# Two matmuls with a gelu between them: contraction rows dealt to partitions in fours, and later transposes

## The chip, the cores and the metric

The kernel runs on one core of one Trainium2 chip. The core has a matrix engine (TensorE, PE in the profile, with its weight loads shown apart as PEld), a vector engine (VectorE, DVE), a scalar engine (ScalarE, ACT), GpSimd (POOL) and SyncE (SP). Data move between the device's memory and the core's on-chip memory by DMA. Two queues issue these DMAs here: SP's, for copies without a change of type, and POOL's, for copies that turn fp32 into bf16 (or to the type fp32r) on the way. The metric is the device time of one execution in microseconds.

## The reference

```python
m, k, n, p = 1024, 1024, 2048, 1024      # a: m x k, b: k x n, c: n x p, all fp32
h = np.matmul(a, b)
h = 0.5 * h * (1 + np.tanh(np.sqrt(2 / np.pi) * (h + 0.044715 * h ** 3)))
return np.matmul(h, c).astype(np.float32)
```

## The kernel before, in words

TensorE multiplies a stationary tile of 128 x 128 (the weights) with a moving tile of 128 x 512; both have the contraction in their 128 partitions. So `h` transposed is computed with tiles of `b` as weights and the transpose of `a` as the moving side: 8 slices of the contraction (`KT`), 16 tiles of columns of `b` (`NT`), and two halves of 512 rows of `a`. Each tile of `h` is the sum of 8 matmuls in one bank of PSUM (the matmul's output memory), and ScalarE takes it through the gelu to on-chip memory. The order of instructions on every engine is the order in which the code writes them.

**First half of the rows.** It has three blocks of columns. *Block 0* is tiles 0 to 5. SP loads `a` by slice (`load_a0`, L74 to L78: 128 or 256 columns of the four row tiles) and `b` by slice (`load_b0`, L80 to L83: 128 rows, 768 columns), in the order of L86 to L89. Per slice, VectorE casts the four 128 x 128 pieces of `a` to bf16 (L107), TensorE transposes them (L110), VectorE copies the result into `aT` (L111), and ScalarE casts the slice of `b` in two halves (L113). The six matmuls of the slice before (`mm0`, L100) stand behind the transposes in TensorE's order. Ten matmuls on zeros (L96) come first of all. *Block 1* is tiles 6 to 9: POOL loads `b` in four DMAs of two slices each (`load_b`, L125 and L130), after a small copy, `gate` (L91), has waited for slice 5 of block 0. *Block 2* is tiles 10 to 15: POOL loads it in four DMAs of four slices and 384 columns, and then the four row tiles of the second half of `a` (L155). `mm1` (L139) computes one tile. After each of the tiles 11 to 14, `turn` (L158) transposes one of the four row tiles, in eight transposes into one PSUM tile and one copy by VectorE (L163). The PSUM tiles of all transposes come from a pool with two buffers (`tpool`).

**Second half of the rows.** The same 16 tiles with `aT[1]`, all data being on chip. POOL loads `c` meanwhile, as four quarters in two DMAs each (L184); `c12` takes the place of `aT[0]`, and so can't be loaded before the first half ends.

**Second product.** It is computed by a scheme of seven block products in place of eight, with sums and differences of blocks of `c` and of `h` that VectorE makes during the second half (`sum_t1`, `sum_t2`, `sum_s1` and others). `t1` uses the buffers of the loaded `a`, `t2` those of the loaded `b`. `prod` (L240) issues eight matmuls per output tile; VectorE combines the results, and SP stores them. The very last output tile is computed in two pieces of 256 columns (L307 to L313).

Where the code names slice `k`, its 128 contraction rows are `k * 128` to `k * 128 + 127`, one in each partition. `b` is addressed through `bv` (L35), and `a` through `av` (L34).

Of the kernel before, what the change touches and what calls it, by code (L numbers as in the profile page):

```python
# [9 lines left out]
F32 = mybir.dt.float32  # L10
BF16 = mybir.dt.bfloat16
F32R = mybir.dt.float32r
SUB = mybir.AluOpType.subtract
ADD = mybir.AluOpType.add
AF = mybir.ActivationFunctionType
# [4 lines left out]
def kernel(ctx, tc, a, b, c, out):  # L20
    nc = tc.nc
    M, K = a.shape
    _, N = b.shape
    _, P = c.shape
    KT = K // 128
    NT = N // 128
    MT = M // 128
    H = 512
    N0 = 6
    W0 = N0 * 128  # L30
    N1 = 4
    W1 = N1 * 128

    av = a.rearrange("(mt p) k -> p mt k", p=128)  # L34
    bv = b.rearrange("(kt p) n -> p kt n", p=128)  # L35
    cv = c.rearrange("(nt p) q -> p nt q", p=128)

    ctx.enter_context(tc.manual_schedule())
    consts = ctx.enter_context(tc.tile_pool(name="consts", bufs=1))
    keep = ctx.enter_context(tc.tile_pool(name="keep", bufs=1))  # L40
    astage = ctx.enter_context(tc.tile_pool(name="astage", bufs=4))
    abf = ctx.enter_context(tc.tile_pool(name="abf", bufs=4))
    b0stage = ctx.enter_context(tc.tile_pool(name="b0stage", bufs=8))
    opool = ctx.enter_context(tc.tile_pool(name="opool", bufs=4))
# [1 line left out]
    tpool = ctx.enter_context(tc.tile_pool(name="tpool", bufs=2, space=PSUM))  # L46
# [3 lines left out]
    ident = consts.tile([128, 128], BF16, name="ident")  # L50
# [3 lines left out]
    aT = [keep.tile([128, KT, H], BF16, name=f"aT{h}", tag=f"A{h}") for h in range(2)]  # L54
    WB = W0 + W1
    b_lo = keep.tile([128, KT, WB], BF16, name="b_lo", tag="B0")
    b_hi = keep.tile([128, KT, N - WB], BF16, name="b_hi", tag="B1")

    def bcols(k0, kn, n0, w):
        if n0 < WB:  # L60
            return b_lo[:, k0:k0 + kn, ds(n0, w)]
        return b_hi[:, k0:k0 + kn, ds(n0 - WB, w)]

    def bt(k, t):
        return bcols(k, 1, t * 128, 128)[:, 0, :]
# [5 lines left out]

    a_st, b_st = {}, {}

    def load_a0(k, n):  # L74
        st = astage.tile([128, 4, 256], F32, name="a_st")
        nc.sync.dma_start(out=st[:, :, 0:n * 128], in_=av[:, 0:4, ds(k * 128, n * 128)])  # L76
        for i in range(n):
            a_st[k + i] = st[:, :, ts(i, 128)]  # L78

    def load_b0(k):  # L80
        st = b0stage.tile([128, W0], F32, name="b0_st")
        nc.sync.dma_start(out=st, in_=bv[:, k, 0:W0])  # L82
        b_st[k] = st  # L83

    gate = consts.tile([128, 1], F32, name="gate")
    for k, n in ((0, 1), (1, 1), (2, 2), (4, 2), (6, 2)):  # L86
        load_a0(k, n)
        for i in range(n):
            load_b0(k + i)  # L89

    nc.gpsimd.tensor_copy(gate, b_st[5][:, 0:1])  # L91
    g = consts.tile([128, 1], F32, name="g")
# [4 lines left out]

    ps = [ppool.tile([128, H], F32, name="ps") for _ in range(N0)]

    def mm0(k):  # L100
        for t in range(N0):
            nc.tensor.matmul(ps[t], bt(k, t), aT[0][:, k, :],  # L102
                             start=(k == 0), stop=(k == KT - 1))

    for k in range(KT):
        ab = abf.tile([128, 4, 128], BF16, name="ab")
        nc.vector.tensor_copy(ab, a_st[k])  # L107
        pt = tpool.tile([128, H], BF16, name="pt")
        for j in range(4):
            nc.tensor.transpose(pt[:, ts(j, 128)], ab[:, j, :], ident)  # L110
        nc.vector.tensor_copy(aT[0][:, k, :], pt)  # L111
        for i in range(2):
            nc.scalar.activation(b_lo[:, k, ts(i, W0 // 2)], b_st[k][:, ts(i, W0 // 2)], AF.Copy)  # L113
        if k > 0:
            mm0(k - 1)
    mm0(KT - 1)

    def gelu(t, h, p):
        nc.scalar.activation(hq[h][t // NH][:, t % NH, :], p, AF.Gelu_apprx_tanh)  # L119
# [3 lines left out]


    def load_b(k0, kn, n0, w):  # L125
        nc.gpsimd.dma_start(out=bcols(k0, kn, n0, w), in_=bv[:, k0:k0 + kn, ds(n0, w)])  # L126

    ps = [(tpool if t < 2 else ppool).tile([128, H], F32, name="pt" if t < 2 else "ps")
          for t in range(N1)]
    for k in range(0, KT, 2):  # L130
        load_b(k, 2, W0, W1)
        for i in range(2):
            for t in range(N1):
                nc.tensor.matmul(ps[t], bt(k + i, N0 + t), aT[0][:, k + i, :],
                                 start=(k + i == 0), stop=(k + i == KT - 1))
# [4 lines left out]
    def mm1(t, h):  # L140
        p = ppool.tile([128, H], F32, name="ps")
        for k in range(KT):
            nc.tensor.matmul(p, bt(k, t), aT[h][:, k, :],  # L143
                             start=(k == 0), stop=(k == KT - 1))
        gelu(t, h, p)

    W2 = 384
    for n0 in range(W0 + W1, N, W2):
        for k in range(0, KT, 4):
            load_b(k, 4, n0, W2)  # L150

    a1 = []
    for j in range(4):
        st = abf.tile([128, K], BF16, name="ab1")
# [3 lines left out]
    def turn(j):  # L158
        ab = a1[j]
        pt = tpool.tile([128, KT, 128], BF16, name="pt")  # L160
        for k in range(KT):
            nc.tensor.transpose(pt[:, k, :], ab[:, ts(k, 128)], ident)  # L162
        nc.vector.tensor_copy(aT[1][:, :, ts(j, 128)], pt)  # L163

    for t in range(N0 + N1, NT):
        mm1(t, 0)
        if NT - 5 <= t < NT - 1:
            turn(t - (NT - 5))

# [5 lines left out]
    c11 = keep.tile([128, NH, H], BF16, name="c11")  # L177
    c21 = keep.tile([128, NH, H], BF16, name="c21")
    c22 = keep.tile([128, NH, H], F32R, name="c22")
    c12 = keep.tile([128, NH, H], BF16, name="c12", tag="A0")  # L180
# [7 lines left out]
    load_c(c21, 1, 0)  # L188
    load_c(c12, 0, 1)

    t1 = [astage.tile([128, 2, H], F32R, name="t1", tag="a_st") for _ in range(4)]
    t2 = [b0stage.tile([128, 1, H], F32R, name="t2", tag="b0_st") for _ in range(8)]
    s1 = keep.tile([128, NH, H], F32R, name="s1")

    def sum_t1(i):
        nc.vector.tensor_tensor(t1[i], c12[:, ts(i, 2), :], c11[:, ts(i, 2), :], op=SUB)  # L196

    def sum_t2(t):
        nc.vector.tensor_tensor(t2[t], c22[:, t:t + 1, :], t1[t // 2][:, t % 2:t % 2 + 1, :], op=SUB)

    def sum_s1(t):
        nc.vector.tensor_tensor(s1[:, t, :], h21[:, t, :], h22[:, t, :], op=ADD)
# [1 line left out]
    for t in range(NT):  # L204
        mm1(t, 1)
        if 3 <= t < 7:
            sum_t1(t - 3)
        if 6 <= t < 10:
            sum_t2(2 * (t - 6))
            sum_t2(2 * (t - 6) + 1)  # L210
        if t == WB // 128:
            t3 = keep.tile([128, NH, H], F32R, name="t3", tag="B0")
        if t >= NH + 1:
            sum_s1(t - NH - 1)
        if WB // 128 <= t < WB // 128 + 4:
            i = t - WB // 128
            nc.vector.tensor_tensor(t3[:, ts(i, 2), :], c22[:, ts(i, 2), :], c12[:, ts(i, 2), :], op=SUB)
# [16 lines left out]
    def sum_t4(t):  # L234
        nc.vector.tensor_tensor(t2[t], t2[t], c21[:, t:t + 1, :], op=SUB)

    def bank(w=H):
        return ppool.tile([128, w], F32, name="ps", padded_shape=[128, H])

    def prod(p, lhs, rhs, j, q=slice(0, H)):  # L240
        for t in range(NH):
            nc.tensor.matmul(p, lhs(t)[:, ts(j, 128)], rhs(t)[:, q],  # L242
                             start=(t == 0), stop=(t == NH - 1))

    def whole(x):
        return lambda t: x[:, t, :]
# [1 line left out]
    def halves(x):  # L248
        return lambda t: x[t // 4][:, t % 4, :]

    def pairs(x):
        return lambda t: x[t // 2][:, t % 2, :]

    def ones(x):
        return lambda t: x[t][:, 0, :]

    def new_out():
        return opool.tile([128, H], F32, name="ot")

    def store(ot, m, q0, w=H):  # L260
        nc.sync.dma_start(out=out[ts(m, 128), ds(q0, w)], in_=ot[:, 0:w])

    def combine(m, q, p, u, op=ADD, swap=False):
        ot = new_out()
        nc.vector.tensor_tensor(ot, u if swap else p, p if swap else u, op=op)  # L265
        store(ot, m, q * H)
# [5 lines left out]
    for j in R:  # L272
        p = bank()
        prod(p, whole(h11), whole(c11), j)
        nc.scalar.activation(u2[j], p, AF.Copy)  # L275
    for j in range(3):
        p = bank()
# [3 lines left out]
    last_keep = opool.tile([128, H], F32, name="lk", bufs=1)  # L281
    nc.gpsimd.tensor_copy(last_keep, last)  # L282
    for j in R:
        p = bank()
        prod(p, halves(s2), ones(t2), j)
        nc.vector.tensor_tensor(u2[j], p, u2[j], op=ADD)
    for j in R:
        p = bank()
# [2 lines left out]
        sum_s4(j)  # L291
    for j in R:
        p = bank()
        prod(p, whole(s1), pairs(t1), j)
        combine(4 + j, 1, p, u3[:, j, :])
        nc.vector.tensor_tensor(u2[j], p, u2[j], op=ADD)
        sum_t4(2 * j)
        sum_t4(2 * j + 1)
    for j in R:
        p = bank()  # L300
        prod(p, halves(s2), whole(c22), j)
        combine(j, 1, p, u2[j])
    for j in R:
        p = bank()
        prod(p, whole(h22), ones(t2), j)
        combine(4 + j, 0, p, u3[:, j, :], op=SUB, swap=True)
    for q in range(2):  # L307
        w = H // 2
        p = bank(w)
        prod(p, whole(h12), whole(c21), 3, q=ds(q * w, w))  # L310
        ot = new_out()
        nc.vector.tensor_tensor(ot[:, 0:w], p, last_keep[:, ds(q * w, w)], op=ADD)  # L312
        store(ot, 3, q * w, w)  # L313

# [1 line left out]
_INS = ['a', 'b', 'c']  # L316
# [26 lines left out]
```

## Time and profile before

| | |
|---|---|
| median of 13 runs | 126.64 us (125.19 to 128.81) |
| time of the profiled execution | 128.38 us |
| its span, first to last instruction | 126.6 us |
| PE busy | 116.6 us (92%) |
| DVE busy | 65.4 us (52%) |
| ACT busy | 29.6 us (23%) |
| DMA of SP's queue (`q1`) | 9.44 MB |
| DMA of POOL's queue (`q0`) | 8.91 MB |

A line of the timeline gives the start and length in microseconds, the engine, the line of the code, the operation, and output and input with the number of instructions; in brackets stands how long the engine was idle before it and what ended that. The chain of work that ended last is followed back from the last instruction, at each step to what released it. A line of the windows gives the busy time of the engines in a stretch, in the order PE, PEld, DVE, ACT, POOL, each with its number of instructions, and then the clock granted to TensorE as a share of the full one, the busy share of the DMA engines and their GB/s.

### The profile page before, as it was taken

What the parts mean: (1) busy time and instruction counts of PE and PEld (TensorE: products, weight loads), DVE (VectorE), ACT (ScalarE), POOL (GpSimd) and SP (SyncE); (2) the same over time, 40 slices, a digit from 0 to 9 for tenths busy, and PEclk for the clock granted to TensorE, in tenths of its full rate; (3) what the DMA queues carried; (4) which work ended last, traced back from release to release, by engine and by line L of the source; (5) the groups of instructions that cost most, each with busy time, mean ns of one, the idle gap of its engine ahead of it and who ended that gap; (6) DMA issues with size and microseconds to landing.
All of it is one profiled execution on the core that took longest, in us unless ns stands there. A gap on an engine that the chain in (4) does not pass through costs nothing.

```text
span 126.6 us, 1439 instructions
## 1 busy us (share of the span) xinstructions
PE 116.6 (92%) x555; PEld 67.6 (53%) x562; DVE 65.4 (52%) x94; ACT 29.6 (23%) x54; POOL 19.9 (16%) x28
## 2 busy tenths in 40 slices
PE   6759999999299999999999999999999999999990
PEld 2224545444045544444444444458888888888860
DVE  0223551000022300008999999997449999974340
ACT  4144456507101322333322333100000000000000
POOL 2000099333440040000000000590000000000000
PEclk9986999999968999999999999999999999999999
DMA  3799999999999999992000000006000022344433
GB/s 111 201 383 377 376 280 155 177 203 204 211 206 206 349 376 216 206 206 42 0 3 0 0 5 0 0 0 224 25 0 0 5 83 83 137 175 185 166 127 122
DMA packets 14245, 18.43 MB, mean 146 GB/s; under 512 B 800, under 2 KB 9760, under 8 KB 14240
## 3 DMA queue, kind: packets, MB, share of 16 engines
q0 software_dynamic: 8000, 8.91, 38.8%
q1 hardware_dynamic: 6240, 9.44, 21.1%
q8 instruction: 4, 0.07, 0.2%
q14 instruction: 1, 0.01, 0.0%
HBM read 20.97 MB, written 4.19 MB: 199 GB/s over the span
## 4 chain that ended last, share of the span: by engine, by line
PE 69%; DMA 18%; POOL 5%; SPq 4%; issue 1%; DVE 0%
PE ps L242 40%; PE ps L143 28%; DMA ab<-in_a_dram 11%; DMA b_st<-in_b_dram 7%; POOL b_lo L126 2%; POOL b_hi L126 2%; SPq L82 2%; SPq L76 2%; PE pt L162 2%; DVE ot L312 0%; POOL gate L91 0%
## 5 line engine op out<-in xcount | busy, mean ns | idle before, releaser
L119 ACT ACTIVATE h<-ps 128x512 fp32r<-128x512 f32 (+1 forms) x30 | 17.3, 602 | 31.4 <-PE ps L143 29.0
L143 PE MATMUL ps<-aT,b_hi 128*128 128x512 bf16 x93 | 23.1, 396 | 0.3 <-issue 0.2
L143 PE MATMUL ps<-aT,b_lo 128*128 128x512 bf16 x79 | 17.4, 379 | 0.1
L143 PEld LDWEIGHTS <-b_hi 128*128 128x128 bf16 x96 | 9.5, 101 | 11.4 <-issue 1.4
L242 PE MATMUL ps<-t,s 128*128 128x512 f32 x64 | 15.1, 393 | 0.0
L242 PE MATMUL ps<-t,h 128*128 128x512 f32 x64 | 14.8, 389 | 0.0
L242 PE MATMUL ps<-c,h 128*128 128x512 bf16 (+1 forms) x71 | 14.1, 355 | 0.1
L163 DVE COPY aT<-pt 128x1024 bf16<-128x1024 bf16 x4 | 2.8, 691 | 21.8 <-PE pt L162 21.8
L242 PEld LDWEIGHTS ps<-t,s 128*128 128x128 f32 x64 | 12.0, 188 | 2.6
L242 PEld LDWEIGHTS ps<-t,h 128*128 128x128 f32 x64 | 12.0, 188 | 2.5
L102 PE MATMUL ps<-aT,b_lo 128*128 128x512 bf16 x47 | 13.0, 417 | 0.1
L143 PEld LDWEIGHTS <-b_lo 128*128 128x128 bf16 x80 | 7.8, 98 | 9.4
L196 DVE TENSOR_TENSOR t<-c,c 128x1024 fp32r<-128x1024 bf16 x4 | 4.7, 1222 | 12.9 <-DMA c<-in_c_dram 12.7
L242 PEld LDWEIGHTS <-h 128*128 128x128 bf16 x72 | 6.9, 98 | 7.0 <-issue 0.3
L282 POOL COPY lk<-u 128x512 f32<-128x512 f32 x1 | 5.1, 5079 | 33.5 <-ACT u L275 33.5
L113 ACT ACTIVATE b_lo<-b_st 128x384 bf16<-128x384 f32 x16 | 7.5, 514 | 10.1 <-DMA b_st<-in_b_dram 9.9
L184 POOL DMA_DIRECT2D c<-in_c_dram x8 | 5.9, 743 | 14.2 <-PE ps L143 8.5
L265 DVE TENSOR_TENSOR ot<-ps,u 128x512 f32<-128x512 f32 x11 | 7.3, 683 | 1.1 <-PE ps L242 1.1
L242 PE MATMUL ps<-c,s 128*128 128x512 f32 x32 | 7.4, 389 | 0.0
L102 PEld LDWEIGHTS <-b_lo 128*128 128x128 bf16 x48 | 4.8, 106 | 4.8 <-issue 1.3
L242 PEld LDWEIGHTS ps<-c,s 128*128 128x128 f32 x32 | 6.0, 188 | 1.2
L111 DVE COPY aT<-pt 128x512 bf16<-128x512 bf16 x8 | 3.4, 424 | 6.3 <-PE pt L110 6.3
(37 smaller groups left out, 92.6 us busy)
## 6 DMA issues: line engine op xcount, KB each, us to landing
out_dram<-ot SPq DMA_DIRECT2D x15, 256.0 KB, 2.1
b_st<-in_b_dram SPq DMA_DIRECT2D x8, 384.0 KB, 8.5
c<-in_c_dram POOLq DMA_DIRECT2D x6, 512.0 KB, 13.4
c<-in_c_dram POOLq DMA_DIRECT2D x2, 1024.0 KB, 14.8
a_st<-in_a_dram SPq DMA_DIRECT2D x3, 512.0 KB, 9.0
b_hi<-in_b_dram POOLq DMA_DIRECT2D x4, 384.0 KB, 11.0
b_lo<-in_b_dram POOLq DMA_DIRECT2D x4, 256.0 KB, 6.3
ab<-in_a_dram POOLq DMA_DIRECT2D x4, 256.0 KB, 13.2
```

The lines of the kernel that those rows point to most:

```text
L102: nc.tensor.matmul(ps[t], bt(k, t), aT[0][:, k, :], start=(k == 0), stop=(k == KT - 1))
L111: nc.vector.tensor_copy(aT[0][:, k, :], pt)
L113: nc.scalar.activation(b_lo[:, k, ts(i, W0 // 2)], b_st[k][:, ts(i, W0 // 2)], AF.Copy)
L119: nc.scalar.activation(hq[h][t // NH][:, t % NH, :], p, AF.Gelu_apprx_tanh)
L126: nc.gpsimd.dma_start(out=bcols(k0, kn, n0, w), in_=bv[:, k0:k0 + kn, ds(n0, w)])
L143: nc.tensor.matmul(p, bt(k, t), aT[h][:, k, :], start=(k == 0), stop=(k == KT - 1))
L163: nc.vector.tensor_copy(aT[1][:, :, ts(j, 128)], pt)
L184: nc.gpsimd.dma_start(out=dst[:, t:t + 4, :], in_=cv[:, r * NH + t:r * NH + t + 4, ts(q, H)])
L196: nc.vector.tensor_tensor(t1[i], c12[:, ts(i, 2), :], c11[:, ts(i, 2), :], op=SUB)
L242: nc.tensor.matmul(p, lhs(t)[:, ts(j, 128)], rhs(t)[:, q], start=(t == 0), stop=(t == NH - 1))
L265: nc.vector.tensor_tensor(ot, u if swap else p, p if swap else u, op=op)
L282: nc.gpsimd.tensor_copy(last_keep, last)
```

## The change

- **Contraction rows dealt in fours.** Slice `k` = 4`g` + `r` now takes the rows 512`g` + 4`p` + `r` for the partitions `p` = 0 to 127. Any assignment of the rows will do as long as `a` and `b` have the same one. For `b` this changes `bv`. For `a` it means that a transpose takes every fourth column of a half row (`strided`).
- **Loads of block 0.** `a` is loaded by half rows: eight DMAs, one per half `g` and row tile `mt`, 128 x 512 elements, into eight buffers for four. They come in another order: the four of the first half, b0, b1, two of the second half, b2, the other two, b3 to b7.
- **Transposes of block 0.** `turn0(g, mt)` casts one such load, transposes its four slices, and copies them to `aT`. All four of the first half precede the first matmul; the four of the second half stand inside the matmuls of slices 1 and 2, after the third and the sixth matmul.
- **Casts of `b` in block 0.** VectorE casts 384 of the 768 columns and ScalarE the others, where ScalarE did both. The casts for slices 2 and 3 are written behind the matmuls and transposes of slices 1 and 2, the others ahead of the slice before.
- **Block 1.** Two DMAs of four slices for four of two.
- **Second half of `a`.** `turn(0)` comes after tile 13 and the other three after tile 14.
- **`t1`** has eight tiles of 512 columns for four of two times 512, and as many subtractions.
- **The last output tile** is cut into 384 and 128 columns.

```diff
-    bv = b.rearrange("(kt p) n -> p kt n", p=128)
+    bv = b.rearrange("(g p r) n -> p g r n", p=128, r=4)
-    astage = ctx.enter_context(tc.tile_pool(name="astage", bufs=4))
+    astage = ctx.enter_context(tc.tile_pool(name="astage", bufs=8))
...
-    def load_a0(k, n):
-        st = astage.tile([128, 4, 256], F32, name="a_st")
-        nc.sync.dma_start(out=st[:, :, 0:n * 128], in_=av[:, 0:4, ds(k * 128, n * 128)])
-        for i in range(n):
-            a_st[k + i] = st[:, :, ts(i, 128)]
+    def load_a0(g, mt):
+        st = astage.tile([128, 512], F32, name="a_st")
+        nc.sync.dma_start(out=st, in_=av[:, mt, ts(g, 512)])
+        a_st[g, mt] = st
...
-        nc.sync.dma_start(out=st, in_=bv[:, k, 0:W0])
+        nc.sync.dma_start(out=st, in_=bv[:, k // 4, k % 4, 0:W0])
...
-    for k, n in ((0, 1), (1, 1), (2, 2), (4, 2), (6, 2)):
-        load_a0(k, n)
-        for i in range(n):
-            load_b0(k + i)
+    for mt in range(4):
+        load_a0(0, mt)
+    load_b0(0)
+    load_b0(1)
+    load_a0(1, 0)
+    load_a0(1, 1)
+    load_b0(2)
+    load_a0(1, 2)
+    load_a0(1, 3)
+    for k in range(3, KT):
+        load_b0(k)
...
-    def mm0(k):
+    def strided(x, r):
+        return x.rearrange("p (c r) -> p r c", r=4)[:, r, :]
+
+    def turn0(g, mt):
+        ab = abf.tile([128, 512], BF16, name="ab")
+        nc.vector.tensor_copy(ab, a_st[g, mt])
+        pt = tpool.tile([128, 4, 128], BF16, name="pt")
+        for r in range(4):
+            nc.tensor.transpose(pt[:, r, :], strided(ab, r), ident)
+        nc.vector.tensor_copy(aT[0][:, ts(g, 4), ts(mt, 128)], pt)
+
+    HW = W0 // 2
+
+    def cast_b0(k):
+        nc.vector.tensor_copy(b_lo[:, k, 0:HW], b_st[k][:, 0:HW])
+        nc.scalar.activation(b_lo[:, k, HW:W0], b_st[k][:, HW:W0], AF.Copy)
+
+    for mt in range(4):
+        turn0(0, mt)
+    cast_b0(0)
+    for k in range(KT):
+        if k + 1 < KT and k not in (1, 2):
+            cast_b0(k + 1)
         for t in range(N0):
             nc.tensor.matmul(ps[t], bt(k, t), aT[0][:, k, :],
                              start=(k == 0), stop=(k == KT - 1))
-
-    for k in range(KT):
-        ab = abf.tile([128, 4, 128], BF16, name="ab")
-        nc.vector.tensor_copy(ab, a_st[k])
-        pt = tpool.tile([128, H], BF16, name="pt")
-        for j in range(4):
-            nc.tensor.transpose(pt[:, ts(j, 128)], ab[:, j, :], ident)
-        nc.vector.tensor_copy(aT[0][:, k, :], pt)
-        for i in range(2):
-            nc.scalar.activation(b_lo[:, k, ts(i, W0 // 2)], b_st[k][:, ts(i, W0 // 2)], AF.Copy)
-        if k > 0:
-            mm0(k - 1)
-    mm0(KT - 1)
+            if k in (1, 2) and t in (2, 5):
+                turn0(1, 2 * (k - 1) + t // 3)
+        if k in (1, 2):
+            cast_b0(k + 1)
...
-        nc.gpsimd.dma_start(out=bcols(k0, kn, n0, w), in_=bv[:, k0:k0 + kn, ds(n0, w)])
+        nc.gpsimd.dma_start(out=bcols(k0, kn, n0, w), in_=bv[:, k0 // 4, k0 % 4:k0 % 4 + kn, ds(n0, w)])
...
-    for k in range(0, KT, 2):
-        load_b(k, 2, W0, W1)
-        for i in range(2):
+    for k in range(0, KT, 4):
+        load_b(k, 4, W0, W1)
+        for i in range(4):
...
-            nc.tensor.transpose(pt[:, k, :], ab[:, ts(k, 128)], ident)
+            nc.tensor.transpose(pt[:, k, :], strided(ab[:, ts(k // 4, 512)], k % 4), ident)
...
-        if NT - 5 <= t < NT - 1:
-            turn(t - (NT - 5))
+        if t == NT - 3:
+            turn(0)
+        if t == NT - 2:
+            turn(1)
+            turn(2)
+            turn(3)
...
-    t1 = [astage.tile([128, 2, H], F32R, name="t1", tag="a_st") for _ in range(4)]
+    t1 = [astage.tile([128, 1, H], F32R, name="t1", tag="a_st") for _ in range(8)]
...
     def sum_t1(i):
-        nc.vector.tensor_tensor(t1[i], c12[:, ts(i, 2), :], c11[:, ts(i, 2), :], op=SUB)
+        for t in (2 * i, 2 * i + 1):
+            nc.vector.tensor_tensor(t1[t], c12[:, t:t + 1, :], c11[:, t:t + 1, :], op=SUB)
...
-    for q in range(2):
-        w = H // 2
+    for q0, w in ((0, 384), (384, 128)):
         p = bank(w)
-        prod(p, whole(h12), whole(c21), 3, q=ds(q * w, w))
+        prod(p, whole(h12), whole(c21), 3, q=ds(q0, w))
         ot = new_out()
-        nc.vector.tensor_tensor(ot[:, 0:w], p, last_keep[:, ds(q * w, w)], op=ADD)
-        store(ot, 3, q * w, w)
+        nc.vector.tensor_tensor(ot[:, 0:w], p, last_keep[:, ds(q0, w)], op=ADD)
+        store(ot, 3, q0, w)
```

## The prediction

> **What bounds the kernel now.** I first read the chain of work that ended last. From 34.83 us on it is TensorE without a break; before that it is a load of `a`:
>
> ```profile
> 21.54 13.29 DMA ab<-in_a_dram
> 34.83 0.05 issue
> 34.88 0.62 PE pt L162 x8
> 35.50 1.11 PE ps L143 x3
> ```
>
> Columns: start, length, what. The transposes of the second half of `a` (L162) wait for a load issued at 21.54. From there to the last matmul TensorE is full, so a shift of the end of the first half (45.05, first weights of the second half) shifts the end by as much.
>
> Second, TensorE's timeline of the start and of that wait:
>
> ```profile
> 5.13 0.39 PE L110 MATMUL pt<-ident,ab 128*128 128x128 bf16 x4
> 7.83 0.40 PE L110 MATMUL pt<-ident,ab 128*128 128x128 bf16 x4 [2.31 <-DVE ab L107]
> 8.07 2.59 PE L102 MATMUL ps<-aT,b_lo 128*128 128x512 bf16 x6
> ...
> 19.26 2.75 PE L102 MATMUL ps<-aT,b_lo 128*128 128x512 bf16 x12
> 21.85 0.59 PE L134 MATMUL pt<-aT,b_lo 128*128 128x512 bf16 x2
> ...
> 34.88 0.62 PE L162 MATMUL pt<-ident,ab 128*128 128x128 bf16 x8 [2.31 <-DMA ab<-in_a_dram]
> ```
>
> The first block runs from 8.07 to 21.85, the second starts at 21.85, and TensorE is idle 2.31 us before 34.88.
>
> Third, windows of 3.41 us around the clock's changes (busy times, then the granted clock):
>
> ```profile
> 4.82:8.24 3.42, 1.11 (x11) 0.64 (x10) 0.85 (x2) 0.94 (x2) 0.00 (x0) 1.00 0.92 302
> 8.24:11.65 3.41, 3.41 (x12) 1.31 (x11) 1.36 (x4) 1.59 (x4) 0.00 (x0) 0.50 1.06 390
> 32.13:35.54 3.41, 1.10 (x12) 0.56 (x10) 0.00 (x1) 0.60 (x1) 1.74 (x3) 1.00 1.13 209
> 35.54:38.96 3.42, 3.20 (x11) 1.48 (x11) 0.69 (x1) 0.18 (x1) 1.06 (x2) 0.50 1.18 206
> ```
>
> Twice a window with TensorE busy 1.1 of 3.4 us is followed by one at half clock. A matmul of 512 columns is then 0.427 us apart from the next, else 0.216 (8 in 1.73), so such a window costs up to 1.7 us.
>
> Fourth, VectorE's timeline, for the change puts work there:
>
> ```profile
> 13.54 0.43 DVE L107 CAST ab<-a_st 128x512 bf16<-128x512 f32 x1
> 14.51 0.42 DVE L111 COPY aT<-pt 128x512 bf16<-128x512 bf16 x1 [0.55 <-PE pt L110]
> 14.85 0.42 DVE L107 CAST ab<-a_st 128x512 bf16<-128x512 f32 x1
> ```
>
> The casts at 13.54 and 14.85 read one and the same load; the second could have run at 13.97, but stands behind the copy, which waits for TensorE. One round is 0.48 (cast to transposes) + 0.43 (to the copy; 0.65 at half clock) + 0.35 (to the next cast) = 1.26 us.
>
> **What the Trainium skill says.** "TensorE: Matmul & The Clock Gate", Part 1, states a free-running window of 3413 ns whose idleness halves the clock; the windows above agree. The same page, "Architectural detail", has VectorE and ScalarE as strict FIFO; the cast at 14.85 agrees. "SBUF — State Buffer", Door 1, has 16-byte lines, read at full rate with two hits per line: a step of four bf16 just keeps that. The clock page, "Weight-path perf modes", allows the fast weight load with a column step. No strided weight load is in this trace.
>
> **The change, part by part.** The sum is against the profiled execution: span 126.6, its time 128.38, so 1.78 around it. The median is 126.64, 1.74 below, about one half-clock window.
>
> *Loads of `a` and `b`.* Four loads of 256 KB (2 KB rows) precede b0, so the first matmul needs 1.05 + 0.39 = 1.44 MB instead of 0.26 + 0.39. The windows of four us moved 131 and 267 GB/s, 0.52 MB by 4 us and 1.59 MB by 8: the 1.44 MB are in by 7.5, about 7.9 with landing; the four `a` loads by 6.7. Total bytes are unchanged. SP issues 16 loads for 13, at 0.33 to 0.85 each, ahead of the data; with eight stage buffers it no longer waits for a cast. Each is needed later than it lands, as follows.
>
> *The start.* All four transpose rounds now precede the first matmul. The first transposes follow the ten warm-up matmuls, at 5.13 as now; copy at 5.56. Then cast 5.91, transposes 6.39, copy 6.82; cast 7.17, transposes 7.65, copy 8.08; cast 8.43, transposes 8.91, copy (half clock) 9.56. Behind it VectorE casts its half of b0 at 9.91: 384 columns, by the row of 0.43 us for 512 with some 0.15 fixed, 0.36 us (0.3 to 0.43). The first matmul starts at 9.91 + 0.36 + 0.05 = 10.3, not 8.07. Needed loads are 1 us or more early, so the VectorE queue sets this, not the DMA.
>
> *Slices 1 to 3.* Nine matmuls (1.94) lead to the first late transposes. From there everything alternates through VectorE's queue, because the cast of b2 stands behind the copy of the second round and that of b3 behind the fourth: copy 0.43, cast 0.35, transposes 0.48, copy 0.43, b2 cast 0.35, matmul 0.41, three matmuls 0.65, copy 0.43, cast 0.35, transposes 0.48, copy 0.43, b3 cast 0.35, matmul 0.41 = 5.55. Slices 3 to 7 are 30 × 0.216 = 6.48. Sum 13.97, of which 48 × 0.216 + 4 × 0.22 = 11.25 are work and 2.7 are new stalls of TensorE. ScalarE has 8 casts for 16 (0.51 each), no gain on this path.
>
> *Clock.* From 5.5 to 10.3 TensorE has three bursts of 0.4 us, as little as the window that lost the clock. It restarts at half clock for 0.6 to 4.0 us by the phase of the window (if some 40% busy releases it; the trace bounds that only between 33% and full): 0.3 to 2.0 us lost, 1.15 taken. The second block starts at 10.3 + 13.97 + 1.15 = 25.4 instead of 21.85.
>
> *Second block of `b`.* POOL issues two loads for four; by the b_hi row 0.79 each against 4 × 0.76, 1.4 us less ahead of the ten that follow. Its gate, b5, has 0.52 MB more ahead of it, up to 1.4 us later; with b6 and b7 (0.79 MB, 2.1 us) still moving the engines stay fed, so what follows lands 0 to 1.4 us later. The present last b_lo load is issued at 17.89 and takes up to 8.3: 26.2, so 26.2 to 27.6 against a need at 25.4 + 3.46 = 28.9. Priced at nothing, covered by TensorE being late; without that cover up to 1.4 us.
>
> *Late transposes.* `turn(0)` comes at 25.4 + 6.91 + 4 × 1.73 = 39.2. Its load lands at 34.83 (to 36.2): the wait of 2.31 and the half clock after it (some 1.8) go. In its place the third of three adjacent turns needs a transpose bank: transposes to copy 0.66, copy 0.69, 0.05, against 0.90 of transposing: 0.5 us of stall. First half ends at 25.4 + 6.91 (32 × 0.216) + 10.37 (48) + 4 × 0.45 + 0.5 = 45.0, against 45.05: 3.6 us lost at the start, 3.6 won here.
>
> *Rest.* t1 in eight tiles: two subtractions pitch 0.61 each for one of 1.18, +0.2 us of VectorE; its s2 sums end at 80.7, over 4 us before TensorE wants them, so nothing (0.2 without that cover). The last store split 384 and 128: final VectorE work 0.29 instead of 0.42, but the store before it (0.33 of SP) now starts 0.35 us before the final one is ready: −0.1 to +0.1, taken 0.
>
> Sum: 128.38 − 0.05 = 128.3 us.
>
> **The rivals.** *Faster:* VectorE's queue is no bound, because casts run ahead of copies. Then the start is the loads': second block at 22.8 (last b_lo load 26.2 less 3.46), first half over at 42.4, 125.7 us. It decides where the second block starts before 23.1. For it: four `ab` buffers and two banks would allow it. Against: the cast at 14.85 kept its place. *Same:* the clock never falls, since bursts of transposes may count differently at another phase: first matmul 10.1, second block 24.1, end 127.0. Against: the window at 4.82. *Slower still:* strided weights load at half rate, as fp32 ones do (188 ns against 98); a transpose would then be 0.11 apart instead of 0.056, 0.22 per group on eight groups and 0.45 on four turns: +3.6, 131.9 at most. *The loads bind:* `b` rows of neighbouring partitions lie 32 KB apart instead of 8; against the needs above they would have to be 2 us later than now, and then cost 1 us, 129.3.
>
> **How the numbers follow.** Likeliest 66%, 128.3, own range 127.5 to 129.1. Faster 9%, 125.7. Same 13%, 127.0 (126.3 to 127.3). Strided loads 8% and late loads 4%, 129.2 to 131.9. The range 127.0 to 129.9 leaves out the faster case, half of the same case, and most of the strided one. A change under 0.5% (126.0 to 127.3) can hardly be told from none: faster 0.09, same 0.13, slower 0.78.
>
> **What the profile after would show.** Right: first matmul of the first block near 10.3 with VectorE, not a DMA, named ahead of it; rounds 1.26 apart; waits of TensorE on VectorE in slices 1 to 3; second block near 25; no wait on `ab` in L162, but about 0.5 us before the last turn. Wrong: casts back to back, transposes longer than 0.45 for eight, or TensorE waiting for `b_st` or `b_lo`. A median under 127.3 would refute the start's price.

## The result and the profile after

The changed kernel is slower: 129.63 us in the median (129.14 to 130.98, 11 runs) against 126.44 us for the kernel before (48 runs), a ratio of 1.0285 with a 95% interval of 1.0253 to 1.0317. Its profiled execution took 130.12 us, with a span of 128.2 us. The forecast had the direction and the mechanism; its size, 128.3 us, was 1.3 us short of the median. Some executions of the kernel before, its profiled one (128.38 us) among them, take about 2 us longer than the others, and the ratios here leave such long executions out.

The chain of work that ended last, in the kernel after (start, length, what). No load stands in it any more; at the start it alternates between TensorE and VectorE:

```profile
6.01 0.42 DVE aT L116
6.43 0.34 DVE ab L112
6.78 0.05 issue
6.83 0.43 PE pt L115 x4
...
10.36 0.36 DVE b_lo L121
10.72 0.05 issue
10.76 4.02 PE ps L131 x9
```

TensorE's timeline after, for the start and for the late transposes:

```profile
5.43 0.54 PE L115 MATMUL pt<-ident,ab 128*128 128x128 bf16 x4
6.83 0.41 PE L115 MATMUL pt<-ident,ab 128*128 128x128 bf16 x4 [0.85 <-DVE ab L112]
8.09 0.42 PE L115 MATMUL pt<-ident,ab 128*128 128x128 bf16 x4 [0.85 <-DVE ab L112]
9.36 0.62 PE L115 MATMUL pt<-ident,ab 128*128 128x128 bf16 x4 [0.85 <-DVE ab L112]
10.76 4.02 PE L131 MATMUL ps<-aT,b_lo 128*128 128x512 bf16 x9 [0.79 <-DVE b_lo L121]
...
17.43 0.82 PE L131 MATMUL ps<-aT,b_lo 128*128 128x512 bf16 x3 [0.90 <-DVE b_lo L121]
...
20.53 6.65 PE L131 MATMUL ps<-aT,b_lo 128*128 128x512 bf16 x30 [0.79 <-DVE b_lo L121]
27.01 0.59 PE L154 MATMUL pt<-aT,b_lo 128*128 128x512 bf16 x2
...
43.00 1.06 PE L182 MATMUL pt<-ident,ab 128*128 128x128 bf16 x16
44.39 0.61 PE L182 MATMUL pt<-ident,ab 128*128 128x128 bf16 x8 [0.34 <-DVE aT L183]
44.84 1.89 PE L163 MATMUL ps<-aT,b_hi 128*128 128x512 bf16 x8
```

The rounds of transposes are 1.26 us apart, each behind a cast of VectorE. The first matmul of block 0 is at 10.76 (8.07 before), block 1 begins at 27.01 (21.85 before), and the transposes of the second half of `a` wait for no load. So 5.16 us are lost up to block 1. From there to the end of the first half nearly 3.9 are won: the matmuls of its last tile begin at 44.84 here, 1.3 us later than in the kernel before:

```profile
43.54 1.89 PE L143 MATMUL ps<-aT,b_hi 128*128 128x512 bf16 x7
```

The windows of 3.41 us around the clock's changes, after (busy time and number on PE, PEld, DVE, ACT, POOL; then the granted clock):

```profile
5.74:9.16 3.42, 1.06 (x12) 0.57 (x9) 2.13 (x6) 0.52 (x1) 0.00 (x0) 1.00 0.98 341
9.16:12.57 3.41, 2.42 (x9) 1.07 (x10) 1.44 (x5) 1.04 (x2) 0.00 (x0) 0.50 1.04 409
12.57:15.98 3.41, 3.41 (x13) 1.37 (x11) 0.73 (x2) 1.04 (x2) 0.00 (x0) 0.50 1.02 398
15.98:19.40 3.42, 2.26 (x16) 1.13 (x16) 1.92 (x6) 1.57 (x3) 3.19 (x5) 1.00 0.71 148
```

The clock was halved for two windows in a row, so the first nine matmuls took 4.02 us. VectorE's timeline after shows why its work stands where it does:

```profile
15.25 0.43 DVE L116 COPY aT<-pt 128x512 bf16<-128x512 bf16 x1 [3.94 <-PE pt L115]
...
16.56 0.42 DVE L116 COPY aT<-pt 128x512 bf16<-128x512 bf16 x1 [0.55 <-PE pt L115]
16.90 0.47 DVE L121 CAST b_lo<-b_st 128x384 bf16<-128x384 f32 x1
17.29 0.41 DVE L112 CAST ab<-a_st 128x512 bf16<-128x512 f32 x1
```

The cast of b2 runs at 16.90 behind a copy. ScalarE began its half of the same slice at 11.89, as soon as the load was in; VectorE's half could have run then too, for VectorE was idle 3.94 us before its copy at 15.25, behind which the cast was written.

### The profile page after: what moved, and what is told of

Same layout as the page of the kernel before. It is cut to its first block, busy times and chain, and to the rows that moved or that the text cites. A ratio compares the mean times of both kernels' runs of the same rounds, so it can differ in the third digit from the quotient of the medians.

```text
span 128.2 us, 1442 instructions
## 1 busy us (share of the span) xinstructions
PE 117.4 (92%) x555; PEld 68.0 (53%) x562; DVE 67.6 (53%) x106; ACT 26.3 (21%) x46; POOL 16.9 (13%) x26
## 4 chain that ended last, share of the span: by engine, by line
PE 91%; DVE 4%; issue 2%; DVEq 0%
PE ps L267 39%; PE ps L163 29%; PE ps L131 10%; PE pt L103 3%; PE ps L154 3%; PE pt L154 3%; PE pt L115 2%; DVE aT L116 2%; PE pt L182 1%; DVE ab L112 1%; DVE b_lo L121 1%; DVE aT L183 1%; DVEq L359 0%; DVE warm L50 0%; DVE ot L333 0%
## 5 line engine op out<-in xcount | busy, mean ns | idle before, releaser
L139 ACT ACTIVATE h<-ps 128x512 fp32r<-128x512 f32 (+1 forms) x30 | 17.3, 602 | 33.8 <-PE ps L163 25.2
L163 PE MATMUL ps<-aT,b_hi 128*128 128x512 bf16 x94 | 21.1, 379 | 0.1
L163 PE MATMUL ps<-aT,b_lo 128*128 128x512 bf16 x78 | 17.3, 379 | 0.1
L267 PE MATMUL ps<-c,h 128*128 128x512 bf16 (+2 forms) x71 | 14.1, 355 | 0.1
L221 DVE TENSOR_TENSOR t<-c,c 128x512 fp32r<-128x512 bf16 x8 | 5.0, 687 | 10.5 <-DMA c<-in_c_dram 10.4
L304 POOL COPY lk<-u 128x512 f32<-128x512 f32 x1 | 3.3, 3309 | 33.5 <-ACT u L297 33.5
L122 ACT ACTIVATE b_lo<-b_st 128x384 bf16<-128x384 f32 x8 | 4.2, 523 | 12.2 <-DMA b_st<-in_b_dram 12.2
```

Source lines behind the costliest of these rows:

```text
L122: nc.scalar.activation(b_lo[:, k, HW:W0], b_st[k][:, HW:W0], AF.Copy)
L163: nc.tensor.matmul(p, bt(k, t), aT[h][:, k, :], start=(k == 0), stop=(k == KT - 1))
L221: nc.vector.tensor_tensor(t1[t], c12[:, t:t + 1, :], c11[:, t:t + 1, :], op=SUB)
L267: nc.tensor.matmul(p, lhs(t)[:, ts(j, 128)], rhs(t)[:, q], start=(t == 0), stop=(t == NH - 1))
```

## The experiments

Each time stands beside runs of the kernel before on the same chip. Their median was 126.87, 126.54 and 127.56 us in the three groups of runs (4, 4 and 2 kernels), so ratios are the safer comparison between groups.

**1. The late transposes alone, in the kernel before.**

```diff
-        if NT - 5 <= t < NT - 1:
-            turn(t - (NT - 5))
+        if t == NT - 3:
+            turn(0)
+        if t == NT - 2:
+            turn(1)
+            turn(2)
+            turn(3)
```

> The kernel before with the late transposes of the second half of a as its only edit. Theory A (TensorE's own work sets the end once the load has landed): the wait of 2.3 us on that load and the half clock after it go, 0.5 us of stall before the last turn comes, so 124.4 to 124.9 us against 126.44; in the profile no wait on the load in front of the transposes. Rival (the late transposes only trade the wait for one on b_hi or on the load of the last row tile): 126.0 to 126.6.

Measured: 125.23 us (124.76 to 125.66), ratio 0.988 (0.9825 to 0.9936). TensorE's timeline of that kernel:

```profile
36.30 0.61 PE L162 MATMUL pt<-ident,ab 128*128 128x128 bf16 x8
38.47 1.06 PE L162 MATMUL pt<-ident,ab 128*128 128x128 bf16 x16
39.86 0.61 PE L162 MATMUL pt<-ident,ab 128*128 128x128 bf16 x8 [0.34 <-DVE aT L163]
```

The wait on the load is gone and the small one on the transpose bank is there. The time is 0.3 us above the range given for theory A and 0.8 us below the rival's. This part of the change is a gain.

**2. The same edit undone in the changed kernel** (the diff above, reversed).

> The changed kernel with its transposes of the second half of a put back after tiles 11 to 14. Theory A (in the changed kernel TensorE is so late that this load has landed anyway): no wait, and the stall of 0.5 us before the last turn goes, so 129.0 to 129.4 us against 129.63. Rival (the late position is what won back 3.9 us of the 5.2 lost at the start): 131.5 us or more.

Measured: 129.03 us (127.16 to 129.38), ratio 1.0102 (0.9964 to 1.0241); the changed kernel has 129.63 and 1.0285. TensorE's timeline:

```profile
36.94 0.61 PE L182 MATMUL pt<-ident,ab 128*128 128x128 bf16 x8
37.39 1.89 PE L163 MATMUL ps<-aT,b_hi 128*128 128x512 bf16 x8
39.11 0.61 PE L182 MATMUL pt<-ident,ab 128*128 128x128 bf16 x8
```

No wait on the load even in the old place, since TensorE comes there at 36.94 and not at 32.6. The rival is out: in the changed kernel the late position wins nothing, and costs its stall of 0.34 us. Not all of the 0.6 us between the times need be that stall: in this execution block 1 also began 0.4 us earlier.

**3. The casts of b2 and b3 ahead, in the changed kernel.**

```diff
-        if k + 1 < KT and k not in (1, 2):
+        if k + 1 < KT:
             cast_b0(k + 1)
...
-        if k in (1, 2):
-            cast_b0(k + 1)
```

> The changed kernel with VectorE's casts of b2 and b3 written ahead of the transposes in slices 1 and 2, not behind them. Theory A (VectorE's order makes the stalls there): two of TensorE's waits of 0.9 and 0.8 us go, block 1 starts at 25.5 to 26.0 instead of 27.0, time 128.2 to 128.7 us. Rival (the half clock alone makes slices 1 to 3 long): 129.4 to 129.8.

Measured: 128.47 us (127.74 to 128.9), ratio 1.0131 (1.0065 to 1.0197). TensorE's timeline:

```profile
19.18 6.64 PE L131 MATMUL ps<-aT,b_lo 128*128 128x512 bf16 x30
25.66 0.59 PE L152 MATMUL pt<-aT,b_lo 128*128 128x512 bf16 x2
```

Slice 3 starts at 19.18 without a wait (20.53 with one), and block 1 at 25.66: theory A, by some 1.2 us.

**4. TensorE kept busy between the groups of transposes, in the changed kernel.**

```diff
     for mt in range(4):
         turn0(0, mt)
+        for _ in range(3):
+            nc.tensor.matmul(ps[mt], warm[:, 0:128], warm, start=True, stop=True)
```

> The changed kernel with three matmuls on zeros behind each of the first four groups of transposes, into a bank that is overwritten later. Theory A (the gaps of 0.85 us between the groups let the clock fall, which then costs 2 us in the first nine matmuls): full clock from 6 us on, the first matmul of block 0 no later than 10.8 and slices 0 and 1 in 2 us instead of 4, time 127.2 to 127.8 us. Rival (the clock falls for another reason, or the extra matmuls only fill time): 129.4 to 130.2.

Measured: 127.44 us (126.72 to 128.28, 20 runs), ratio 1.0099 (1.007 to 1.0127). TensorE's timeline, and then the windows around it:

```profile
8.73 0.81 PE L127 MATMUL ps<-warm 128*128 128x512 bf16 x3
9.68 2.12 PE L133 MATMUL ps<-aT,b_lo 128*128 128x512 bf16 x9
...
23.68 0.59 PE L156 MATMUL pt<-aT,b_lo 128*128 128x512 bf16 x2
```

```profile
3.96:7.37 3.41, 3.00 (x21) 1.34 (x20) 1.52 (x4) 0.00 (x0) 0.00 (x0) 1.00 0.95 316
7.37:10.78 3.41, 3.07 (x20) 1.26 (x19) 2.14 (x6) 1.04 (x2) 0.00 (x0) 1.00 1.00 336
```

Twelve matmuls that compute nothing make the kernel 2.2 us faster. The nine matmuls take 2.12 us for 4.02, and the clock stays full. In this execution the warm-up matmuls also ended earlier (first transposes at 4.71 instead of 5.43), so not all of the 3.3 us up to block 1 is due to the added ones.

**5. VectorE's whole queue reordered, in the changed kernel.** Nothing is added. At the start each cast of `a` stands one copy further ahead, and in slices 0 to 2 the casts of `a` and `b` stand ahead of the copies that wait for TensorE.

```diff
-    for mt in range(4):
-        turn0(0, mt)
+    cast_a(0, 0)
+    cast_a(0, 1)
+    turn0(0, 0)
+    cast_a(0, 2)
+    turn0(0, 1)
+    cast_a(0, 3)
+    turn0(0, 2)
+    turn0(0, 3)
     cast_b0(0)
     for k in range(KT):
-        if k + 1 < KT and k not in (1, 2):
+        if k + 1 < KT:
             cast_b0(k + 1)
+        if k == 0:
+            cast_a(1, 0)
+            cast_a(1, 1)
...
             if k in (1, 2) and t in (2, 5):
                 turn0(1, 2 * (k - 1) + t // 3)
+                if k == 1:
+                    cast_a(1, 2 + t // 3)
-        if k in (1, 2):
-            cast_b0(k + 1)
```

Here `cast_a` is the first, and `turn0` the rest, of the old `turn0`.

> The changed kernel with VectorE's work in another order: at the start each cast of a is written ahead of the copy of the round before, and in slices 0 to 2 the casts of a and b are written ahead of the copies. Nothing else is changed. Theory A (the queue of VectorE, not the loads, set the start): first matmul at 9.0 to 9.3 us instead of 10.8, no wait of TensorE on a cast of b longer than the load of that b explains, block 1 starts at 22 to 23.5 instead of 27.0, time 125 to 126.5 us against 129.63. Rival (the loads set it too, since b0 lands only after four loads of a): first matmul later than 10 and 128 us or more.

Measured: 124.97 us (124.41 to 125.44), ratio 0.9882 (0.9831 to 0.9933): from 2.9% slower to 1.2% faster than the kernel before, with the same loads, the same casts and the same rows. TensorE's timeline:

```profile
5.43 1.06 PE L119 MATMUL pt<-ident,ab 128*128 128x128 bf16 x8
...
9.34 3.72 PE L144 MATMUL ps<-aT,b_lo 128*128 128x512 bf16 x9 [0.79 <-DVE b_lo L125]
...
15.81 6.64 PE L144 MATMUL ps<-aT,b_lo 128*128 128x512 bf16 x30
22.35 0.61 PE L167 MATMUL pt<-aT,b_lo 128*128 128x512 bf16 x2
```

The first two groups of transposes follow each other, the stalls in slices 1 to 3 are gone, and block 1 starts at 22.35, not 27.01. The first matmul came at 9.34, 0.04 us past the range, and the time is 0.03 us below its own. So VectorE's order is shown as the cause of the late start and of the stalls. Part of the 4.7 us is the clock, which comes back one window earlier here, and the experiment does not separate the two. The rival has a share as well once the order is mended, for the third round now waits for its load:

```profile
6.99 0.43 DVE L114 CAST ab<-a_st 128x512 bf16<-128x512 f32 x1 [0.46 <-DMA a_st<-in_a_dram]
```

**6. The reordered queue and the filling matmuls together.** As in 5, with three, two and four matmuls on zeros behind the second, third and fourth group of transposes.

> As the one with the casts ahead, and nine matmuls on zeros between the first groups of transposes, into banks that are overwritten later. Theory A (what is left of the loss at the start is the clock): block 1 starts at 20 to 22, bound now by its own load, and the time is 124.3 to 125.3 us, at or below the kernel before with late transposes alone. Rival (clock of no importance once the casts run ahead): within 0.4 us of the one without these matmuls.

Measured: 125.97 us (124.61 to 128.65, 20 runs), ratio 0.994 (0.9909 to 0.9971), above the range given, so neither side. In the profiled execution the clock is full and the 30 matmuls of slices 3 to 7 start at 14.87, but block 1 then waits:

```profile
14.87 6.65 PE L151 MATMUL ps<-aT,b_lo 128*128 128x512 bf16 x30 [0.22 <-DVE b_lo L125]
22.27 0.61 PE L174 MATMUL pt<-aT,b_lo 128*128 128x512 bf16 x2 [0.76 <-DMA b_lo<-in_b_dram]
```

The load of block 1 takes what the clock gave: block 1 starts at 22.27, as in 5, and both spans are 123.5 us. So the filling pays only while TensorE is the late one. The median is above that of 5, but the intervals of the two ratios overlap, and this execution does not explain the difference. One possibility, argued only, is that where the warm-up leaves the clock low the nine added matmuls take twice as long.

**7. The first part of the change alone.** The edit of 1 in the kernel before, and block 1 in two loads:

```diff
-    for k in range(0, KT, 2):
-        load_b(k, 2, W0, W1)
-        for i in range(2):
+    for k in range(0, KT, 4):
+        load_b(k, 4, W0, W1)
+        for i in range(4):
```

> The kernel before with late transposes and block 1 loaded in two DMAs of four slices: the first part of the change alone, without the dealt rows and what goes with them. Theory A (the second part alone makes the changed kernel slower): 124.8 to 125.6 us, as with the late transposes alone, since TensorE reaches the first load at 22 us, about when it lands. Rival (the larger loads make TensorE wait at block 1): 126 us or more.

Measured: 124.59 us (123.92 to 124.79), ratio 0.9844 (0.9794 to 0.9895). By the two ratios this is 1.6% faster than the kernel before and some 4% faster than the changed one, and the lowest median found, though its interval overlaps those of 1 and 5. Block 1 starts without a wait on the larger load:

```profile
22.09 0.59 PE L134 MATMUL pt<-aT,b_lo 128*128 128x512 bf16 x2
```

The first part is a gain, and what makes the changed kernel slower came with the second.

**8. The last output tile in even pieces, in the changed kernel** (256 and 256 for 384 and 128).

> The changed kernel with its last output tile cut into 256 and 256 columns, as before. Theory A (384 and 128 put the last subtraction and the last store behind their forerunners, by 0.3 us): from the last matmul to the end of the span 3.5 us instead of 3.85, time 0.3 us below the changed kernel, 129.3. Rival (the smaller last piece pays): equal or 0.1 to 0.3 us above it.

Measured: 129.81 us (126.99 to 130.5), against 129.63. Five of the six executions took 129.26 us or more and one 126.99, so no gain of 0.3 us shows, but the times alone do not rule it out. The close does. From the end of the last matmul to the landing of the last store it took 2.35 us here (124.03 to 126.38), 2.34 in the changed kernel (124.52 to 126.86) and 2.34 before (123.22 to 125.56), so the cut neither costs nor gains. The difference comes after that landing: 1.32 or 1.33 us to the end of the span in all eight traces of the changed kernel and its variants, 1.01 or 1.02 in all four of the kernel before and its variants. There SyncE works through eight semaphore instructions, one every 0.06 us, in each of the eight traces, and through three in each of the four; the five more are the 0.3 us. Why there are eight is open.

**9. The filling cut to five matmuls and block 1 in four loads again,** otherwise as in 6.

> The changed kernel with the casts ahead, five matmuls on zeros instead of nine between the groups of transposes, and block 1 loaded in four DMAs of two slices again. Theory A (with the start repaired, block 1 waits for its first load, which lands earlier in the small form): block 1 starts at 21 to 21.8 us without a wait on its load, time 124.0 to 124.8. Rival (the smaller loads only slow what follows): 125 to 126.

Measured: 125.74 us (124.52 to 127.36, 20 runs), ratio 0.9945 (0.9912 to 0.9979). A miss: the time is the rival's. TensorE's timeline:

```profile
20.72 0.59 PE L174 MATMUL pt<-aT,b_lo 128*128 128x512 bf16 x2
...
23.82 0.60 PE L174 MATMUL pt<-aT,b_lo 128*128 128x512 bf16 x2 [1.21 <-DMA b_lo<-in_b_dram]
```

Block 1 starts at 20.72 without a wait, and then waits 1.21 us for the second of the small loads, which landed at 23.77. The one large load of 6, which holds as much as these two, had landed at 22.23. Two things were changed from 6, so the times do not show what each is worth; they hardly differ (125.97 and 125.74).

**10. Half of each cast of `b` on VectorE, added to 7,** behind the copy of the same slice.

> The kernel before with the first part of the change (late transposes, block 1 in two loads), and VectorE casting half of each slice of b behind the copy of the same slice, as the second part has it. Theory A (the last slices of block 0 wait for the casts of their b, which are 0.45 us shorter): block 1 starts 0.2 to 0.5 us earlier, time 124.1 to 124.5. Rival (VectorE's order makes the next cast of a late): 124.9 or more.

Measured: 125.26 us (125.1 to 126.41), ratio 0.9886 (0.976 to 1.0012). The time is the rival's, though the interval takes in that of 7, so the times do not show a loss. VectorE's timeline of that kernel shows the order that the rival speaks of:

```profile
18.63 0.59 DVE L112 CAST b_lo<-b_st 128x384 bf16<-128x384 f32 x1
19.14 0.41 DVE L107 CAST ab<-a_st 128x512 bf16<-128x512 f32 x1
```

The last cast of `a`, whose load was in before 17.3 (its twin was cast from it then), stands behind a cast of `b`. From the cast of slice 6 to block 1 it is 5.14 us here (17.29 to 22.43) and 4.87 in the trace of 7 (17.22 to 22.09), some 0.3 us that this order can account for.

## Why the prediction was right in kind and short in size

**Right.** VectorE's queue sets the start: rounds of 1.26 us were forecast and measured, and experiment 5 shows the cause, since another order of the same work takes 4.7 us off (the clock's share in that included). The stalls at b2 and b3 were forecast at 2.7 us in all; in the trace after, VectorE's casts of `b` and `a` hold TensorE there for 0.90, 0.20 and 0.79 us, while part of this stretch, up to 15.98, ran at half clock and shows fewer waits. The 30 matmuls from slice 3 on take the 6.48 us given, and the way from block 1 to the end of the first half is 19.55 us for the 19.58 of the sum. The loads were no bound, though later than forecast: b0 landed at 8.57 and not by 7.9, and its cast began at 10.36. The first load for the late transposes landed at 34.39, 6 us before its use, and the stall before the last turn came (0.34 us for 0.5). The rival that casts overtake copies was no property of the hardware, but as an edit of the order (experiment 5) it gives 124.97, near the 125.7 priced for it.

**The terms that were mis-sized,** in the sum for the profiled execution (128.3 against 130.12):

- *Clock.* "It restarts at half clock for 0.6 to 4.0 us" was 5.2 us, from 10.76 to 15.98. The window in which the matmuls began was busy 2.42 of 3.41 us and did not release the clock; I had taken some 40% to be enough. The nine matmuls took 4.02 us where the sum has 1.94 + 1.15: +0.93, and the chain behind them 5.74 for 5.55: +0.19. By experiment 4 the whole clock is worth about 2.2 us. This is the step that failed: the time at half clock was put too short.
- *Start.* The first copy came at 6.01, not 5.56, because the ten warm-up matmuls ended later (first transposes in the timeline at 5.43, not 5.13). I had copied the kernel before, where a later end of the warm-up is hidden by the wait for a load. Here it is on the path: +0.46 at the first matmul.
- *The close.* "Taken 0": from the last subtraction to the end of the span 3.3 us instead of 2.9, and 0.14 more around the span (1.92 for 1.78). The split of the last tile, the only thing that the prediction weighed there, does not explain it. It is the five more semaphore instructions of SyncE after the last store has landed (experiment 8). They go with the three more DMAs on SP's queue; the reason is open.

These make 1.59 at block 1 and about 0.5 at the close. Against them stand 0.2, since I measured the end of the first half at the first weights (45.05) and not at the first matmul (45.26).

**The gain put on the late transposes.** "3.6 won here" was right as a difference between the two traces and wrong as the worth of the edit. Experiment 2 shows that the changed kernel loses the wait without it. Some 1.7 of the 3.6 were half clock after the wait, which the profiled execution before had and its median, 1.74 lower, mostly has not: of the executions of the kernel before in the experiments, 20 of the 21 with a mean clock of 0.973, which is that of the profiled one, took 127.9 us or more, and 27 of the 29 at 1.0 took less than 127.2. This did not enter the size, because the end at 45.0 was summed up from the work of the changed kernel. The size of the change, 1.3% forecast against 2.85%, is short by the terms above and by 0.2 us more, the median of the kernel before being 126.44 and not 126.64.

## What to carry to other kernels

On an engine that works strictly in order, a cast that feeds the matrix engine should stand ahead of a copy that waits for it; one round of cast, transpose and copy in series was 1.26 us here, and four of them ahead of the first matmul, with the clock that fell meanwhile, made the kernel slower although its loads were in time. Even with the order mended (experiment 5, ratio 0.988) no gain shows over the late transposes alone (experiment 1, 0.988). A gain that is read off a wait is worth only what is left when the work in front of it is late: the same edit gave 1.2% in one kernel and nothing in the other. Where several edits come together, run the parts apart: the first part of this change alone has the lowest median found.

## What was not expected of the hardware

- **How busy a window had to be.** At full clock, windows with TensorE busy 1.06 of 3.42 us (after, from 5.74) and 1.39 of 3.41 (experiment 5) were followed by half clock, and windows with 1.73 and 1.78 (experiment 7, 5.15 to 11.98) kept the full one. At half clock, 2.42 of 3.41 did not release it (after, from 9.16); 2.94 did, in experiment 8. The lines are those of experiment 5 and, last, of 8:

```profile
6.28:9.69 3.41, 1.39 (x13) 0.74 (x12) 2.36 (x7) 0.52 (x1) 0.00 (x0) 1.00 1.03 365
9.69:13.10 3.41, 3.41 (x12) 1.31 (x10) 1.57 (x4) 1.05 (x2) 0.00 (x0) 0.50 1.04 407
...
10.18:13.59 3.41, 2.94 (x7) 1.04 (x8) 1.02 (x4) 0.68 (x2) 0.00 (x0) 0.50 1.04 412
```

  In busy time these are two marks. They need not be two thresholds: a matmul at half clock takes 0.427 us for 0.216, and if what counts is the work done, 2.42 and 2.94 are worth half, 1.21 and 1.47. One mark between 1.39 and 1.47 then fits all of these windows. The runs do not decide between the two, nor what transposes count for: all of the 1.06 us and 0.62 of the 2.42 are transposes.

  The Trainium skill, "TensorE: Matmul & The Clock Gate", Part 1, speaks of an idle window that lowers the clock and a busy one that releases it. Here a window that was busy for 41%, transposes included, was followed by half clock, and one busy for 71% at half clock did not release it.
- **Strided weights cost next to nothing.** A weight load that takes every fourth bf16 lasted 114 to 116 ns in the median instead of 98, and four transposes took 0.39 to 0.42 us at full clock, as before (0.39 to 0.40); the rival that priced them like fp32 loads (188 ns) is out.
- **Smaller loads only moved the wait.** In the changed kernel with its start mended and four loads of two slices, block 1 starts without a wait and then stands 1.21 us for the second of them (experiment 9); with two of four slices it waits 0.76 us at its start (experiment 6).
